# A Conformer convolution's taps moved from GpSimd to VectorE, with its place, its memory and the order of four merges changed

## The chip, the cores and the metric

The kernel runs on one core of one Trainium2 chip. The time is that of one execution on the device, in microseconds, from the slowest (here the only) core; lower is better. Of the engines, TensorE (PE) multiplies matrices into PSUM, VectorE (DVE), ScalarE (ACT) and GpSimd (POOL) work element by element, and SyncE (SP) issues most of the DMAs. Each engine takes its instructions in the order in which the built program has them, and waits on semaphores for the others.

## The reference, cut to what matters

One layer of a trunk, 256 latent and 256 context tokens, 2048 channels. One wide input projection feeds four parallel token mixers of 512 channels; their outputs are projected back, weighted with sigmoid gates, added, and sent through one output projection. A gated ConvFFN follows.

```python
def conv_module(u, p):
    a, gte = jnp.split(u, 2, axis=-1)
    y = a * jax.nn.sigmoid(gte)
    y = dwconv1d(y, p['conv_dw']) + p['conv_b']          # 31 taps, 512 channels, 256 tokens
    y = layer_norm(y, p['conv_ln_g'], p['conv_ln_b'], NORM_EPS)
    return jax.nn.silu(y)

def merge_branches(ys, gate_cols, w_br, w_out):
    ys = jnp.stack([y.astype(dt) for y in ys], axis=2)   # convolution, mLSTM, DeltaNet, RWKV
    br = jnp.einsum('btnw,nwd->btnd', ys, w_br)
    gates = jax.nn.sigmoid(gate_cols.reshape(*gate_cols.shape[:2], N_BRANCH, -1))
    return jnp.sum(gates * br, axis=2) @ w_out
```

The four branches enter a sum, so the order in which they are merged is free.

## The kernel before

**Matrix products.** Every product with a large weight is made from three matmuls. A block of weights of 256 rows and 512 columns (512 KB) comes by DMA into a tile `raw` (four buffers, `load_split`, L194). ScalarE rounds it to a tile `hi` (L198), VectorE writes the remainder into a tile `lo` (L200, called "a `lo`" below), and TensorE adds hi with hi, hi with lo and lo with hi of the activations `uh` and `ul`, which all go through the helper line L79. `hi` and `lo` have two buffers each. So a step of a weight product can only start when VectorE has written its `lo`. The PSUM tile of a product that has the tokens as rows is named `psA`, with the tokens as columns `psB`; a pool of four banks (`mmp`) holds them.

**The order of the work.** The code is written function by function, and the build then places every instruction in a fixed order for each engine by a simulated timeline; work written later goes forward into gaps of work written earlier, where its data and its memory allow it. So the function that is written first has precedence, not the right to finish first. In the region that the change touches, `build` writes: `rw_out` (RWKV output), `gd_scan` and `gd_out` (the DeltaNet scan and its output), `conv_module`, `ml_scan` (the mLSTM scan with its output), `gates` (the 8192 gate columns, 128 steps of 12 matmuls, no dependence on the scans), four calls of `merge` (branch 3 RWKV, 0 convolution, 2 DeltaNet, 1 mLSTM), `out_proj`, then the FFN. The gates are TensorE's filler for the three scans. The columns of the adaLN projection (`w_mod`, PSUM tile `psw`) are fed in between by `feed`, a fraction of a step after each step of the products; they read one buffer `wraw`.

**conv_module.** The padded input `cpad` is loaded, and four blocks of 128 channels get 31 taps of 256 tokens each into `cacc`. Blocks 0 and 1 are on VectorE, one multiply-add for each tap (L869). Blocks 2 and 3 are on GpSimd, a multiply (L874) and an add (L875) for each tap. Then come the layer norm, whose means over channels are matmuls with a matrix of ones (`pscm`, `pscv`), SiLU, and `put_y` (L778, L779), which splits the result into `uh` and `ul` for the merge.

**The DeltaNet scan** inverts a triangular matrix for each segment and direction: first two small steps (L417, L418), then fifteen rounds of a shuffle (L434), a product (`gim`, L402) and an addition (L403) on VectorE, then a reset (L427). Its masks are made on GpSimd (`gdr`).

**The mLSTM scan** takes four heads and two directions. For each, TensorE makes the exponents' argument (`psr`), ScalarE five exponentials (`mA`, L1254 to L1259), VectorE three products, TensorE the sums (`psn`), and VectorE the quotient (`mlh`). Then `head_out` normalises and splits.

**merge** multiplies one branch by its 2048 columns of `w_br` in four blocks of 512, reads the gates back from DRAM (`sig`), and adds up in `mg`; VectorE multiplies, GpSimd adds (L1347).

**Memory.** Pools are stacks from both ends of the SBUF, and a tile that takes over an address waits until the tile before it there was read for the last time. Before, the mLSTM scan's pool `mrp` (addresses 174144 to 221568) lies over the convolution's pool `cvp` (182912 to 194656), and `mg` lies over the mLSTM tiles `mA`.

Of the kernel before, what the change touches and what calls it, by code (L numbers as in the profile page):

```python
# [11 lines left out]
F32 = mybir.dt.float32  # L12
# [3 lines left out]
AF = mybir.ActivationFunctionType  # L16
ALU = mybir.AluOpType
# [3 lines left out]
P = 128  # L21
D = 2048
# [19 lines left out]
class Kern:  # L42
# [812 lines left out]
    def conv_module(self):  # L855
        nc, PC = self.nc, self.PC
        cp = self.cvp
        cpad = cp.tile([P, 4, 286], F32, name="cpad")
# [3 lines left out]
        acc = cp.tile([P, 4, 256], F32, name="cacc")  # L862
        w = lambda i, t: PC["conv_dw"][:, 4 * t + i : 4 * t + i + 1]
        for i in range(4):
            a = acc[:, i]
            if i < 2:
                nc.vector.tensor_scalar(a, cpad[:, i, 0:256], w(i, 0), PC["conv_b"][:, i : i + 1], ALU.mult, ALU.add)
                for t in range(1, 31):
                    nc.vector.scalar_tensor_tensor(a, cpad[:, i, t : t + 256], w(i, t), a, ALU.mult, ALU.add)  # L869
            else:  # L870
                nc.gpsimd.tensor_scalar(a, cpad[:, i, 0:256], w(i, 0), PC["conv_b"][:, i : i + 1], ALU.mult, ALU.add)
                for t in range(1, 31):
                    m = cp.tile([P, 256], F32, tag="ctap", name="ctap", bufs=2)
                    nc.gpsimd.tensor_scalar(m, cpad[:, i, t : t + 256], w(i, t), None, ALU.mult)  # L874
                    nc.gpsimd.tensor_tensor(a, a, m, ALU.add)  # L875
        ps = self.aux("pscm")
# [5 lines left out]
        for i in range(4):  # L882
            nc.vector.tensor_tensor(acc[:, i], acc[:, i], mean, ALU.subtract)
            sq = cp.tile([P, 256], F32, tag="ctap", name="csq", bufs=2)
            nc.gpsimd.tensor_tensor(sq, acc[:, i], acc[:, i], ALU.mult)
            self.mm(ps2[:, 0:256], self.ones, sq, start=i == 0, stop=i == 3)
# [132 lines left out]
    def gd_scan(self):  # L1019
# [4 lines left out]
        wp = self.pool("gwp", bufs=2, stack=ges, side="right")  # L1024
        self.G[0] = self.pool("g1p", stack=self.ues).tile([P, D], F32, name="G1")
        tp = self.pool("gtp", stack=ges, side="right")
# [156 lines left out]
    def ml_scan(self):  # L1183
# [4 lines left out]
        wp = self.pool("mwb", bufs=2, stack=self.mlx)  # L1188
        mqT, mkT = mp.tile([P, 4, 256], F32, name="mqT"), mp.tile([P, 4, 512], F32, name="mkT")
        mv = mp.tile([P, 4, 4, 132], F32, name="mv")  # L1190
# [354 lines left out]
    def build(self):  # L1545
# [46 lines left out]
        res.close()  # L1592
        ces = ExitStack()
        self.gop = self.pool("gop", stack=ces, side="right")
        self.cvp = self.pool("cvp", stack=ces, side="right")
        self.gd_scan()
        self.gd_out()
        self.conv_module()
        ces.close()
        self.ml_scan()  # L1600
        self.gates()
        self.feed(96)
        self.rate = 0.0
        fes.close()
        self.dbg("yh", self.uh[:, :, 0:256].bitcast(F32))
        self.dbg("yl", self.ul[:, :, 0:256].bitcast(F32))
        self.mgw = self.pool("mgw", bufs=3, stack=ues)
        self.mgp = self.pool("mgp", stack=ues)
        self.mg = self.mgp.tile([P, 2, D], F32, name="mg")
        self.hlp = self.pool("hlp", bufs=2, stack=ues)  # L1610
        self.resp = self.pool("resp", side="right")
        self.x1 = self.resp.tile([P, 2, D], F32, name="x1")
        self.ffdw = self.resp.tile([P, 396], F32, name="ffdw")
        self.nc.sync.dma_start(out=self.ffdw, in_=self.A["taps"])
        for i, n in enumerate((3, 0, 2, 1)):
            self.merge(i == 0, n)
# [69 lines left out]
```

## Time and profile before

| what | us |
|---|---|
| median of 3 runs | 2329.57 (2326.28 to 2334.89) |
| the profiled execution | 2329.05 |
| its span, first to last instruction | 2327.1 |
| granted TensorE clock, mean of the span | 0.977 |
| taps on VectorE (L869), first to last start | 789.1 to 848.7 |
| taps on GpSimd (L874), first to last start | 789.0 to 947.7 |
| means of the convolution (`pscm`), first start | 1210.6 |
| its last split (`ul`, L779), start | 1233.1 |

The stages in the span: RWKV scan and the columns of the branches up to some 765 us, the gates with the three scans up to 1317, the four merges from 1342 to 1454, the output projection to 1521, and the FFN to the end. The profile's page gives the shares of the engines and the span in 40 slices of 58 us; a question about less than such a slice goes to the windows, the timeline and the groups of instructions, which the prediction quotes. Busy time of TensorE is modelled (matmuls overlap), so a short wait can be hidden in it.

### The profile page before, as it was taken

To read this page: it belongs to the slowest core of one execution; us is meant where nothing else is said; L and a number is where in the kernel's file an instruction comes from. 1 tells how busy PE (TensorE), PEld (TensorE's weight loads), DVE (VectorE), ACT (ScalarE), POOL (GpSimd) and SP (SyncE) were. 2 spreads that over 40 slices of the span, in tenths; PEclk is the share of its full clock that TensorE was granted. 3 is DMA by queue.
4 is the path that set the end of the run, shared out by engine and by line. 5 is a ranking of instruction groups with operands and counts; after the bars stand their busy time and mean duration, and the time that the engine had idled before them with its cause. 6 is when DMAs were issued, how large, how long until landed. Compare 5 with 4: busy or idle time off the path is not lost.

```text
span 2327.1 us, 42867 instructions
## 1 busy us (share of the span) xinstructions
PE 2215.9 (95%) x16828; PEld 1812.0 (78%) x16828; DVE 1449.6 (62%) x3027; ACT 989.5 (43%) x1493; POOL 507.6 (22%) x865
## 2 busy tenths in 40 slices
PE   6979889999999989999999899989999999999998
PEld 3657667877888666777777678779999999998886
DVE  3357766734555678457565476577776677775554
ACT  4225644533554344334236434444443444444443
POOL 0012553533454599210010033010000000000000
PEclk8989999999999999999999999989999999999999
DMA  9934663555666776787777476567677666666663
GB/s 369 352 115 127 170 183 113 159 171 170 199 188 180 231 208 209 231 247 237 226 231 256 139 257 217 181 231 222 212 222 217 202 182 183 179 205 202 194 193 101
DMA packets 273867, 471.97 MB, mean 203 GB/s; under 512 B 41761, under 2 KB 80929, under 8 KB 272673
## 3 DMA queue, kind: packets, MB, share of 16 engines
q1 hardware_dynamic: 273378, 467.14, 64.8%
q8 instruction: 132, 2.16, 0.4%
q10 hardware_dynamic: 288, 2.10, 0.2%
q14 instruction: 69, 0.57, 0.1%
HBM read 440.33 MB, written 28.84 MB: 202 GB/s over the span
## 4 chain that ended last, share of the span: by engine, by line
PE 78%; DVE 8%; DMA 7%; POOL 4%; ACT 2%; issue 2%; SPq 0%; DVEq 0%; ACTq 0%; POOLq 0%
PE psB L79 37%; PE psA L79 18%; PE psD L79 10%; PE psw L79 4%; DMA wraw<-in_w_mod 3%; DVE lo L200 2%; POOL ctap L874 1%; DMA raw<-in_w_mix 1%; PE psG L79 1%; POOL cacc L875 1%; ACT hi L198 1%; PE psn L79 1%; DMA raw<-in_w_in 1%; PE psf L79 1%; DVE cacc L869 1%
## 5 line engine op out<-in xcount | busy, mean ns | idle before, releaser
L200 DVE TENSOR_TENSOR lo<-raw,hi 128x1024 fp32r<-128x1024 f32 (+2 forms) x485 | 599.2, 1236 | 458.7 <-ACT hi L198 450.0
L198 ACT ACTIVATE hi<-raw 128x1024 fp32r<-128x1024 f32 (+2 forms) x488 | 509.2, 1045 | 796.5 <-PE psB L79 348.6
L79 PE MATMUL psB<-u2h,hi 128*128 128x256 f32 x1408 | 399.5, 286 | 1.2 <-DVE u2h L1370 1.2
L79 PE MATMUL psB<-u2l,hi 128*128 128x256 f32 x1408 | 398.8, 284 | 0.5 <-DVE u2l L1371 0.5
L79 PE MATMUL psB<-u2h,lo 128*128 128x256 f32 x1408 | 399.0, 284 | 0.0
L79 PE MATMUL psA<-lo,uh 128*128 128x512 f32 x832 | 337.4, 406 | 18.4 <-DVE lo L200 18.0
L79 PE MATMUL psA<-hi,ul 128*128 128x512 f32 x832 | 332.7, 400 | 0.0
L79 PE MATMUL psA<-hi,uh 128*128 128x512 f32 x832 | 311.4, 405 | 3.2 <-DVE mg L1344 2.1
L79 PE MATMUL psB<-uh,hi 128*128 128x256 f32 (+1 forms) x832 | 281.0, 346 | 18.7 <-ACT hi L198 16.4
L79 PE MATMUL psB<-ul,hi 128*128 128x256 f32 (+2 forms) x832 | 278.5, 339 | 0.0
L79 PEld LDWEIGHTS psB<-u2h,hi 128*128 128x128 f32 x1408 | 269.6, 192 | 10.9 <-issue 9.5
L79 PEld LDWEIGHTS psB<-u2l,hi 128*128 128x128 f32 x1408 | 270.5, 192 | 0.7 <-DVE u2l L1371 0.7
L79 PE MATMUL psB<-uh,lo 128*128 128x256 f32 (+2 forms) x832 | 263.0, 339 | 8.1 <-DVE lo L200 8.1
L79 PEld LDWEIGHTS psB<-u2h,lo 128*128 128x128 f32 x1408 | 270.5, 192 | 0.1
L79 PEld LDWEIGHTS psA<-lo,uh 128*128 128x128 f32 x832 | 158.1, 190 | 68.5 <-DVE lo L200 27.5
L79 PEld LDWEIGHTS psB<-uh,hi 128*128 128x128 f32 x832 | 158.6, 191 | 51.2 <-ACT hi L198 18.5
L79 PEld LDWEIGHTS psA<-hi,uh 128*128 128x128 f32 x832 | 154.7, 190 | 53.2 <-issue 12.2
L79 PEld LDWEIGHTS psA<-hi,ul 128*128 128x128 f32 x832 | 158.3, 190 | 36.5 <-issue 2.6
L79 PEld LDWEIGHTS psB<-uh,lo 128*128 128x128 f32 (+1 forms) x832 | 152.8, 189 | 32.0 <-DVE lo L200 10.5
L79 PEld LDWEIGHTS psB<-ul,hi 128*128 128x128 f32 (+1 forms) x832 | 157.8, 190 | 23.1 <-issue 6.4
L1541 DVE TENSOR_TENSOR lo<-raw,hi 128x1024 fp32r<-128x1024 f32 x88 | 107.7, 1226 | 78.5 <-ACT hi L1540 78.5
L1461 DVE SCALAR_TENSOR_TENSOR facc<-fpad,ffdw,facc 128x256 f32<-128x256 f32 x352 | 152.8, 490 | 0.2
(573 smaller groups left out, 3028.8 us busy)
## 6 DMA issues: line engine op xcount, KB each, us to landing
raw<-in_w_in SPq DMA_DIRECT2D x208, 512.0 KB, 4.3
raw<-in_ffn_up SPq DMA_DIRECT2D x176, 512.0 KB, 3.8
wraw<-in_w_mod SPq DMA_DIRECT2D x160, 512.0 KB, 5.1
raw<-in_ffn_down SPq DMA_DIRECT2D x88, 512.0 KB, 4.5
raw<-in_w_br SPq DMA_DIRECT2D x32, 512.0 KB, 5.1
raw<-in_w_out SPq DMA_DIRECT2D x32, 512.0 KB, 4.4
raw<-in_w_mod SPq DMA_DIRECT2D x32, 512.0 KB, 3.8
raw<-in_w_in SPq DMA_DIRECT2D x48, 256.0 KB, 4.1
```

The costliest lines, as they stand in the source:

```text
L79: self.nc.tensor.matmul(out, lhsT, rhs, start=start, stop=stop)
L198: nc.scalar.activation(hi[s], raw[s], AF.Copy)
L200: (nc.gpsimd if self.pool_lo >= 0 else nc.vector).tensor_tensor(lo[s], raw[s], hi[s].bitcast(F32), ALU.subtract)
L869: nc.vector.scalar_tensor_tensor(a, cpad[:, i, t : t + 256], w(i, t), a, ALU.mult, ALU.add)
L874: nc.gpsimd.tensor_scalar(m, cpad[:, i, t : t + 256], w(i, t), None, ALU.mult)
L875: nc.gpsimd.tensor_tensor(a, a, m, ALU.add)
L1461: nc.vector.scalar_tensor_tensor(s3(acc), pad[:, dy : dy + 4, dx : dx + 64], tap(t, b), s3(acc), ALU.mult, ALU.add)
L1541: nc.vector.tensor_tensor(f(lo), f(raw), f(hi).bitcast(F32), ALU.subtract)
```

## The change

All four blocks of taps are one multiply-add for each tap on VectorE; GpSimd keeps none. The squares for the variance move from GpSimd to ScalarE. `conv_module` is written behind `gates` instead of behind `gd_out`, its pool stays open until then, and the merges run in the order 3, 2, 1, 0, so that the convolution's branch comes last. In memory, `mqT` and `mkT` of the mLSTM scan get a pool of their own, G1 (the gain of the first residual) is allocated behind the mLSTM scan and not in the DeltaNet scan, `resp` and `hlp` are opened ahead of the merge buffers, and `ffdw` is eight columns wider. The addresses that follow: `mrp` lies at 190560 to 225696 and `cvp` at 178816 to 190560, apart from each other; `x1` (from 178304) now lies over `cvp`.

```diff
@@ conv_module
-            if i < 2:
-                nc.vector.tensor_scalar(a, cpad[:, i, 0:256], w(i, 0), PC["conv_b"][:, i : i + 1], ALU.mult, ALU.add)
-                for t in range(1, 31):
-                    nc.vector.scalar_tensor_tensor(a, cpad[:, i, t : t + 256], w(i, t), a, ALU.mult, ALU.add)
-            else:
-                nc.gpsimd.tensor_scalar(a, cpad[:, i, 0:256], w(i, 0), PC["conv_b"][:, i : i + 1], ALU.mult, ALU.add)
-                for t in range(1, 31):
-                    m = cp.tile([P, 256], F32, tag="ctap", name="ctap", bufs=2)
-                    nc.gpsimd.tensor_scalar(m, cpad[:, i, t : t + 256], w(i, t), None, ALU.mult)
-                    nc.gpsimd.tensor_tensor(a, a, m, ALU.add)
+            nc.vector.tensor_scalar(a, cpad[:, i, 0:256], w(i, 0), PC["conv_b"][:, i : i + 1], ALU.mult, ALU.add)
+            for t in range(1, 31):
+                nc.vector.scalar_tensor_tensor(a, cpad[:, i, t : t + 256], w(i, t), a, ALU.mult, ALU.add)
...
-            nc.gpsimd.tensor_tensor(sq, acc[:, i], acc[:, i], ALU.mult)
+            nc.scalar.activation(sq, acc[:, i], AF.Square)
@@ gd_scan
-        self.G[0] = self.pool("g1p", stack=self.ues).tile([P, D], F32, name="G1")
@@ ml_scan
-        mqT, mkT = mp.tile([P, 4, 256], F32, name="mqT"), mp.tile([P, 4, 512], F32, name="mkT")
+        qk = self.pool("mqk", stack=self.mlx)
+        mqT, mkT = qk.tile([P, 4, 256], F32, name="mqT"), qk.tile([P, 4, 512], F32, name="mkT")
@@ build
         ces = ExitStack()
+        cvs = ExitStack()
+        self.cvp = self.pool("cvp", stack=cvs, side="right")
         self.gop = self.pool("gop", stack=ces, side="right")
-        self.cvp = self.pool("cvp", stack=ces, side="right")
         self.gd_scan()
         self.gd_out()
-        self.conv_module()
         ces.close()
         self.ml_scan()
+        self.G[0] = self.pool("g1p", stack=ues).tile([P, D], F32, name="G1")
         self.gates()
         self.feed(96)
         self.rate = 0.0
+        self.conv_module()
+        cvs.close()
         fes.close()
...
+        self.resp = self.pool("resp", side="right")
+        self.hlp = self.pool("hlp", bufs=2, stack=ues)
         self.mgw = self.pool("mgw", bufs=3, stack=ues)
         self.mgp = self.pool("mgp", stack=ues)
         self.mg = self.mgp.tile([P, 2, D], F32, name="mg")
-        self.hlp = self.pool("hlp", bufs=2, stack=ues)
-        self.resp = self.pool("resp", side="right")
         self.x1 = self.resp.tile([P, 2, D], F32, name="x1")
-        self.ffdw = self.resp.tile([P, 396], F32, name="ffdw")
-        self.nc.sync.dma_start(out=self.ffdw, in_=self.A["taps"])
-        for i, n in enumerate((3, 0, 2, 1)):
+        self.ffdw = self.resp.tile([P, 404], F32, name="ffdw")
+        self.nc.sync.dma_start(out=self.ffdw[:, 0:396], in_=self.A["taps"])
+        for i, n in enumerate((3, 2, 1, 0)):
             self.merge(i == 0, n)
```

What the build makes of it is seen in three places. First VectorE under the taps, between the first and the second `royf` rows of the RWKV output and on. Before (`x6` is six rows of the kind in a row):

```order
L1312 TENSOR_TENSOR royf<-royf,psgo 128x256
L869 SCALAR_TENSOR_TENSOR cacc<-cpad,vec,cacc 128x256 x3
L200 TENSOR_TENSOR lo<-raw,hi 128x1024
L779 TENSOR_TENSOR ul<-royf,uh 128x256
L869 SCALAR_TENSOR_TENSOR cacc<-cpad,vec,cacc 128x256 x6
L200 TENSOR_TENSOR lo<-raw,hi 128x1024
L869 SCALAR_TENSOR_TENSOR cacc<-cpad,vec,cacc 128x256 x2
L1312 TENSOR_TENSOR royf<-royf,psgo 128x256
L869 SCALAR_TENSOR_TENSOR cacc<-cpad,vec,cacc 128x256 x4
L200 TENSOR_TENSOR lo<-raw,hi 128x1024
L869 SCALAR_TENSOR_TENSOR cacc<-cpad,vec,cacc 128x256
```

In the change, from the first `ul` row of the RWKV output on:

```order
L779 TENSOR_TENSOR ul<-royf,uh 128x256
L868 SCALAR_TENSOR_TENSOR cacc<-cpad,vec,cacc 128x256 x3
L288 TENSOR_TENSOR mod_139<-psf,vec 128x2 x2
L200 TENSOR_TENSOR lo<-raw,hi 128x1024
L868 SCALAR_TENSOR_TENSOR cacc<-cpad,vec,cacc 128x256 x3
L1305 TENSOR_TENSOR royf<-royf,psgo 128x256
L868 SCALAR_TENSOR_TENSOR cacc<-cpad,vec,cacc 128x256 x3
L200 TENSOR_TENSOR lo<-raw,hi 128x1024
L868 SCALAR_TENSOR_TENSOR cacc<-cpad,vec,cacc 128x256 x2
L779 TENSOR_TENSOR ul<-royf,uh 128x256
L868 SCALAR_TENSOR_TENSOR cacc<-cpad,vec,cacc 128x256 x4
```

The taps stand among the `lo` rows in both, at the same place in the program. In the change they go on longer: the last tap stands behind the 24th `lo` from the first tap on, where before the first step of the DeltaNet inverse stands behind the 22nd.

Second, TensorE behind the DeltaNet output (`psho`). Before, the convolution's means come next:

```order
L79 MATMUL psA<-lo,uh 128x512
L79 MATMUL psA<-hi,ul 128x512
L79 MATMUL psA<-hi,uh 128x512
L79 MATMUL psho<-ident,go 128x2x64 x2
L79 MATMUL pscm<-cacc,ones 128x256 x4
L79 MATMUL psA<-lo,uh 128x512
L79 MATMUL psA<-hi,ul 128x512
L79 MATMUL psA<-hi,uh 128x512 x2
```

In the change, at the same place:

```order
L79 MATMUL psA<-hi,ul 128x512
L79 MATMUL psA<-hi,uh 128x512
L79 MATMUL psA<-lo,uh 128x512
L79 MATMUL psho<-ident,go 128x2x64 x2
L90 MATMUL psml<-ident,li 4x128 x4
L79 MATMUL psw<-wraw,cst 32x256
L90 MATMUL psml<-ident,spx 4x128 x4
L79 MATMUL psw<-wraw,cst 32x256 x3
```

The mLSTM scan's preparation (`psml`) stands directly behind the DeltaNet output, between steps of `w_mod`, and the convolution's means stand in the merges, behind the mLSTM output.

Third, TensorE at the end of the mLSTM scan, from where the first two blocks of the merge of branch 3 have been multiplied. Before:

```order
L79 MATMUL psq_11528<-mqT,mkT 128x256 x2
L79 MATMUL psn<-mv,mA 128x129 x5
L79 MATMUL psq_11529<-mqT,mkT 128x256 x2
L79 MATMUL psr<-mlr_11292,mlsel 128x256 x2
L79 LDWEIGHTS idb
L79 MATMUL psr<-mlmask,idb 128x256
L79 MATMUL psn<-mv,mA 128x129 x7
L79 MATMUL psr<-mlr_11324,mlsel 128x256 x2
L79 LDWEIGHTS idb
L79 MATMUL psr<-mlmask,idb 128x256
L79 MATMUL psn<-mv,mA 128x129 x7
L79 MATMUL psA<-hi,uh 128x512
```

In the change:

```order
L79 MATMUL psA<-hi,ul 128x512
L79 MATMUL psr<-mlr_10998,mlsel 128x256 x2
L79 LDWEIGHTS idb
L79 MATMUL psr<-mlmask,idb 128x256
L79 MATMUL psw<-wraw,cst 32x256 x4
L79 MATMUL psf<-wrows,selb 128x256 x2
L79 MATMUL psn<-mv,mA 128x129 x7
L79 MATMUL psr<-mlr_11030,mlsel 128x256 x2
L79 LDWEIGHTS idb
L79 MATMUL psr<-mlmask,idb 128x256
L79 MATMUL psn<-mv,mA 128x129 x7
L79 MATMUL psA<-hi,uh 128x512
```

Before, three pairs of a `psr` and the `psn` that needs it are left when the merge has no free PSUM bank (the `psr` of the first stands three rows ahead of this piece); in the change two are left, and the last step of `w_mod` stands among them.

## The prediction

> **What bounds the kernel now.** The profile's page comes first, for the share of each engine, then the table of windows, for the stages that the change touches.
>
> ```profile
> PE 2215.9 (95%) x16828; PEld 1812.0 (78%) x16828; DVE 1449.6 (62%) x3027; ACT 989.5 (43%) x1493; POOL 507.6 (22%) x865
> ```
>
> TensorE is busy for 95% of the span, so a change that moves no matmul work off it can win only time in which it waits, or runs at a lowered clock. In the windows the columns are length, PE, PEld, DVE, ACT and POOL busy, granted clock, DMA share, GB/s:
>
> ```profile
> 788.00:885.00 97.00, 86.14 (x492) 60.09 (x491) 77.21 (x114) 37.23 (x51) 93.13 (x91) 0.96 0.72 211
> 885.00:938.00 53.00, 46.47 (x400) 32.06 (x400) 49.94 (x152) 20.42 (x27) 49.64 (x51) 0.96 0.70 209
> 938.00:961.00 23.00, 22.43 (x263) 16.47 (x263) 8.51 (x9) 9.19 (x13) 7.51 (x9) 0.94 0.77 228
> 961.00:1308.00 347.00, 344.15 (x2510) 253.51 (x2506) 202.10 (x445) 144.67 (x194) 26.13 (x27) 1.00 0.77 234
> 1308.00:1342.00 34.00, 24.74 (x112) 19.11 (x110) 13.15 (x33) 10.63 (x28) 0.70 (x1) 0.80 0.27 95
> 1342.00:1373.00 31.00, 29.27 (x120) 22.68 (x121) 23.94 (x43) 11.02 (x13) 7.45 (x6) 0.94 0.74 269
> ```
>
> While the taps run (788 to 938) TensorE idles 10.9 + 6.5 us, 0.6 more to 961, and its clock is lowered by 4 to 6%, which is 3.9 + 2.1 + 1.4 = 7.4 us of clock. After that it waits 2.9 us in 347: there nothing is to be won. The hole from 1308 to 1342 (the end of the mLSTM scan) holds 9.3 us of idling, the first merges 1.7.
>
> **Why TensorE idles under the taps.** Two groups of VectorE work between 788 and 850, two of GpSimd between 780 and 960 (busy, mean ns):
>
> ```profile
> L869 DVE SCALAR_TENSOR_TENSOR cacc<-cpad,vec,cacc 128x256 f32<-128x256 f32 x60 | 38.5, 684 | 0.0
> L200 DVE TENSOR_TENSOR lo<-raw,hi 128x1024 fp32r<-128x1024 f32 x14 | 19.5, 1395 | 0.0
> L874 POOL TENSOR_SCALAR ctap<-cpad,vec 128x256 f32<-128x256 f32 x60 | 76.8, 1289 | 0.0
> L875 POOL TENSOR_TENSOR cacc<-cacc,ctap 128x256 f32<-128x256 f32 x60 | 55.9, 931 | 1.7
> ```
>
> VectorE holds the 60 taps of two channel blocks and the `lo` halves without which the gates' matmuls cannot start. GpSimd takes 132.7 us for the other 60. A tap costs VectorE 38.5/60 = 0.64 us here. In the FFN, where GpSimd rests, the same operation of the same size looks like this (start, length of the merged run), and below it the same 56-element step of the DeltaNet inverse (in the tile name `gim`), first with GpSimd's taps running, then without:
>
> ```profile
> 1572.71 1.22 DVE L200 TENSOR_TENSOR lo<-raw,hi 128x1024 fp32r<-128x1024 f32 x1
> 1573.85 1.27 DVE L1461 SCALAR_TENSOR_TENSOR facc<-fpad,ffdw,facc 128x256 f32<-128x256 f32 x3
> ...
> 1588.96 2.47 DVE L1461 SCALAR_TENSOR_TENSOR facc<-fpad,ffdw,facc 128x256 f32<-128x256 f32 x6
> 899.46 0.74 DVE L402 TENSOR_TENSOR gim<-gib,giU 128x56 f32<-128x56 f32 x1
> 1061.52 0.21 DVE L402 TENSOR_TENSOR gim<-gib,giU 128x56 f32<-128x56 f32 x1
> ```
>
> Three more taps take 2.47 - 1.27 = 1.20 us, so a tap costs 0.40 us, and a `lo` costs 1573.85 - 1572.71 = 1.14 us. A step of 0.21 us takes 0.74 us beside GpSimd. So the two engines hold each other up, and the taps slow VectorE even where they run on GpSimd. The Trainium skill, page "SBUF — State Buffer", section "Who interferes with whom", says that a VectorE instruction with two SBUF inputs and a GpSimd instruction that reads SBUF shut each other out for a whole instruction. By that rule GpSimd's other work in the three windows, 150.3 - 132.7 = 17.6 us, would go on blocking VectorE, and term A below would be anything up to 17.6 us less; by the rows it is as below, and I keep the rows.
>
> **Term A, the taps (788 to 961).** By the order of the built programs the taps still start at the same place, not behind the gates. 60 taps join VectorE, 120 operations leave GpSimd. Up to the first step of the inverse, at 884.90 in this trace, VectorE had 22 `lo` rows; in the change it has 24, two steps of the gates further.
>
> ```profile
> 884.90 0.36 DVE L417 TENSOR_SCALAR giA<-giC,mlo 128x128 f32<-128x128 f32 x1 [0.31 <-ACT giC L94]
> 910.53 0.18 DVE L427 COPY giU<-I 128x128 f32<-128x128 f32 x1
> 1050.24 0.29 DVE L417 TENSOR_SCALAR giA<-giC,mlo 128x128 f32<-128x128 f32 x1 [0.78 <-ACT giC L94]
> 1069.06 0.19 DVE L427 COPY giU<-I 128x128 f32<-128x128 f32 x1
> 1378.52 33.51 PE psA L79 x144
> ```
>
> - VectorE's sum: 120 x 0.40 + 24 x 1.14 + 4 opening taps at 0.40 + the rest of that stretch, about 77.2 - 38.5 - 19.5 - 8 x 1.3 = 9 us: 48.0 + 27.4 + 1.6 + 9 = 86 us, so 874.
> - TensorE's sum: 86.1 us busy, less the 3.9 of lowered clock, plus two steps of 12 matmuls at 33.51/144 = 0.233 us (the chain of waits), 5.6 us: 87.8 us, so 876.
>
> The two are nearly equal and take turns, so I put the inverse at 880: 4.9 us earlier and 5.6 us of gates further, 10.5 us. The first inverse took 910.53 - 884.90 = 25.6 us against 18.8 us in the second segment, where GpSimd is quiet. There TensorE becomes the limit (46.5 us busy, 2.1 of them lowered clock, in 53), and I count 5 us for both directions. **Term A is -15 us.** Its ends: all idling and all lowered clock go, -18.0 - 7.4 = -25; or a tap still costs 0.64 us, then VectorE has 115 us to the inverse, which starts at 903 with 5.6 us of gates more done: +12.5.
>
> **Term B, the end of the mLSTM scan.** It has two parts. First, in the old layout the scan's memory lay over the convolution's:
>
> ```profile
> POOL mv L1191 <- DVE ul L779: 13.9, 1, 13.9
> 1317.12 1.13 PE L79 MATMUL psr<-mlr,mlsel 4*128 4x256 f32 x4
> 1325.83 0.45 PE L79 MATMUL psr<-mlr,mlsel 4*128 4x256 f32 x1 [0.60 <-DVE mlh L1280]
> 1332.65 2.04 PE L79 MATMUL psr<-mlr,mlsel 4*128 4x256 f32 x4 [1.47 <-DVE mlh L1278]
> 1342.25 0.50 PE L79 MATMUL psA<-hi,uh 128*128 128x512 f32 x1 [2.09 <-DVE mg L1344]
> 1320.28 1.20 PE L79 MATMUL psn<-mv,mA 128*128 128x129 f32 x4 [1.82 <-DVE mA L1261]
> ```
>
> GpSimd's `mv` waited 13.9 us for the last `ul` of the convolution, and the scan's loads stand behind it. In the change the scan starts right behind the DeltaNet output. Second, the merge of branch 3 fills four PSUM banks and then stops until the scan is over; three psr-to-psn pairs are left at that point before, two in the change. The first of the three runs from 1317.12 to 1325.83, 8.7 us, but its matmuls are not saved, they move into the busy gates. What goes is its idling, 1.8 + 0.6 = 2.4 us. **Term B is -2.5 us**; at best the whole 8.7 us, at worst nothing, if the scan is late by its own chain.
>
> **Term C, the convolution's ending.** Means, squares, reciprocal, SiLU and splits leave the stage with 2.9 us of idling in 347 and come into the first merges:
>
> ```profile
> 1213.06 2.27 DVE L883 TENSOR_TENSOR cacc<-cacc,cmean 128x256 f32<-128x256 f32 x4 [0.75 <-ACT cmean L880]
> 1222.24 1.28 ACT L888 ACT_TABLE_LOAD   x1
> 1224.69 1.75 DVE L889 RECIPROCAL crt<-crt 128x256 f32<-128x256 f32 x1 [1.21 <-ACT crt L888]
> 1226.55 1.43 DVE L891 TENSOR_TENSOR cacc<-cacc,crt 128x256 f32<-128x256 f32 x4
> 1226.63 1.28 ACT L892 ACT_TABLE_LOAD   x1
> 1357.12 2.12 ACTq L1420 DMA_DIRECT2D x<-in_x  x2
> 1359.53 10.60 DMA raw<-in_w_br
> ```
>
> With four splits of 0.33 that is 2.27 + 1.75 + 1.43 + 1.3 = 6.8 us of VectorE, put where VectorE is busy 23.9 of 31 us already: 30.7. The cover is nearly used up. The squares move from GpSimd to ScalarE, which has room there (11.0 of 31). The 2 MB of `x` are queued on ScalarE behind this ending, since `x1` now lies over the convolution's memory; today they collide with the merges' weights (10.6 us for a load at 1359), later they will again. SP's loads of `w_mod` move too: more of them stand between the last gate weights and the first merge weights. They run in the scan's hole, where the DMA share is 0.27, so I count nothing for them, at most one load. Ends: 0, if the 7 us of VectorE slack are enough; +9.4, if 6.8 us and both table loads are exposed. I take **+3 us**, nearer the rows that say there is room. The new place of G1, the wider `ffdw` and the order of merges 2, 1 and 0 issue the same instructions at the same prices: 0.
>
> **The sum.** -15 - 2.5 + 3 = -14.5 us on the profiled execution of 2329.05 us (span 2327.1), which is 0.5 us from the median of the runs: 2314.5, and I forecast **2314 us**. 0.5% is 11.6 us, about what a measurement of this kernel can tell from no change.
>
> **The rivals.**
> - *VectorE becomes the bound (slower).* The taps cost 0.64 us whatever GpSimd does. Then A is +12.5, and the sum 2329 + 12.5 - 2.5 + 3 = 2342. The point from which A turns is where 788.3 + 38 + 120 taps reaches 884.9 + 5.6: 0.535 us a tap. For it: VectorE is the saturated engine (no idling in the 62 us to 850). Against it: 0.40 us in the FFN, 0.21 against 0.74 us in the inverse. The Trainium skill, page "Perfetto Trace Analysis", section "Optimizing Scalar/DVE Operations", advises giving work of a saturated VectorE away, even to GpSimd, and so speaks against this change; it adds that the shared port may undo that, and the 0.74 us row sides with the second half.
> - *Only the inverse gains.* VectorE and TensorE do not take turns well while the taps run, and 10.9 us of idling stay: A is -5 - 2.5 of clock, the sum 2329 - 7.5 - 2.5 + 3 = 2322.
> - *The merges give it back.* C is +9.4: 2329 - 15 - 2.5 + 9.4 = 2321. For it: the 30.7 of 31 us. Against it: the ending spreads over some 13 steps of 2.8 us.
> - *All of it goes.* A -25, C 0: 2329 - 25 - 2.5 = 2301.5.
>
> **How the numbers follow.** Forecast 0.50 (its own range 2308 to 2319), only the inverse 0.16, the merges 0.16, all of it 0.10, VectorE bound 0.08. Faster by over 0.5% (below 2317.9): 0.45 of the forecast, 0.10 of the best case, 0.04 of the two middle ones, 0.59. Slower by over 0.5%: 0.07. Within: 0.34. The range that leaves out about 2 in 10 runs from 2303, near the best case, to 2327, above the middle ones.
>
> **What would show it.** Taps at 0.40 us and inverse steps near 0.2 us; the inverse starting near 880 with 24 `lo` before it; idling from 788 to 961 down from 18 to some 8 us, clock near 0.98; `mv` no longer waiting for `ul`; two pairs in the hole; and in the 31 us behind it VectorE near 30 with TensorE idling some 4 us in place of 1.7. It is wrong if a tap takes over 0.53 us, or if the merges' `lo` rows come later than every 2.8 us.

## The result, and the profile after

The changed kernel takes **2315.48 us** (median of 4 runs, 2314.22 to 2316.15) beside 2328.28 us of the kernel before; the ratio is **0.9944** with a 95% interval of 0.9932 to 0.9957. A second set of six runs gave 0.9943 (0.9926 to 0.9959). So it is faster by 13 us, about 0.56%, and the interval reaches to both sides of the 0.5% that was named as the bound. The forecast was 2314 us.

First the share of each engine on the page of the changed kernel, then its windows, with the columns of before; the first three are the stretches that the prediction quoted.

```profile
PE 2216.0 (96%) x16828; PEld 1810.1 (78%) x16828; DVE 1448.9 (63%) x3089; ACT 990.7 (43%) x1498; POOL 374.2 (16%) x739
```
```profile
788.00:885.00 97.00, 93.90 (x558) 66.83 (x557) 94.11 (x186) 40.98 (x55) 21.54 (x25) 1.00 0.80 249
885.00:938.00 53.00, 51.08 (x554) 36.95 (x553) 39.35 (x150) 23.20 (x30) 1.09 (x3) 1.00 0.81 249
938.00:961.00 23.00, 23.00 (x205) 16.57 (x205) 9.97 (x17) 9.94 (x15) 0.00 (x0) 1.00 0.75 216
961.00:1283.50 322.50, 320.76 (x2306) 234.24 (x2303) 186.77 (x423) 130.88 (x175) 18.80 (x22) 1.00 0.74 226
1283.50:1318.24 34.74, 28.10 (x142) 21.13 (x141) 14.02 (x29) 12.70 (x26) 2.22 (x2) 0.85 0.58 186
1318.24:1433.90 115.66, 111.02 (x491) 89.51 (x492) 85.66 (x118) 51.83 (x74) 42.65 (x28) 0.99 0.69 234
```

Under the taps TensorE now idles 3.1 + 1.9 + 0 = 5.0 us in place of 18.0, and GpSimd is busy for 22.6 us in place of 150.3. The last two rows are the hole from the last gate to the restart of the merges, and the merges up to the output projection. The same two stretches before (there the gates end at 1300.1; what TensorE multiplies from then to 1317 are mostly the first blocks of the merge of branch 3):

```profile
1300.10:1342.25 42.15, 32.64 (x153) 25.85 (x152) 16.33 (x39) 14.26 (x33) 0.95 (x1) 0.84 0.38 125
1342.25:1451.70 109.45, 107.87 (x476) 86.62 (x477) 76.97 (x105) 43.76 (x58) 41.71 (x26) 0.98 0.74 247
```

The hole is shorter (34.7 after 42.2 us), the merges are longer (115.7 after 109.5), and TensorE idles in them 4.6 us in place of 1.6. From these and the later milestones of the two traces the difference adds up:

| up to | before | after | step |
|---|---|---|---|
| restart of the merges (first `psA` behind the hole) | 1342.25 | 1318.24 | -24.0 |
| first `mg` of the output projection | 1451.7 | 1433.9 | +6.2 |
| last residual of the attention half (`x`, an1ry) | 1526.2 | 1510.3 | +1.9 |
| end of the span | 2327.1 | 2313.7 | +2.5 |

24 us are won before the merges, and 10.6 are given back behind them: in the merges, and, unexpectedly, in the output projection and the FFN. A second profiled execution of the same program has +0.5 and +1.0 us in these last two rows in place of +1.9 and +2.5, so a part of them is chance: in the output projection the granted clock was 0.97 in the first execution and 1.00 in the second.

The taps and the inverse in the changed kernel: a group of VectorE from 788 to 884, two single rows, and a group from 885 to 905 (busy, mean ns).

```profile
L868 DVE SCALAR_TENSOR_TENSOR cacc<-cpad,vec,cacc 128x256 f32<-128x256 f32 x120 | 57.1, 524 | 0.0
```
```profile
883.57 0.28 DVE L417 TENSOR_SCALAR giA<-giC,mlo 128x128 f32<-128x128 f32 x1 [1.44 <-ACT giC L94]
902.49 0.19 DVE L427 COPY giU<-I 128x128 f32<-128x128 f32 x1
L402 DVE TENSOR_TENSOR gim<-gib,giU 128x120 f32<-128x120 f32 (+14 forms) x16 | 3.5, 220 | 0.0
```

A tap costs VectorE 57.1/120 = 0.476 us (0.64 before, 0.40 predicted). The inverse starts at 883.6, with the predicted 24 `lo` rows ahead of it, and its first piece takes 902.49 - 883.57 = 18.9 us in place of 25.6. GpSimd's `mv` now waits for the end of the DeltaNet output (`psho`) and not for the convolution's `ul`:

```profile
L1184 POOL MEMSET mv<- x1: 127/127/127, 1191.5 to 1191.5; 128x16 f32 x1
its engine sat idle before it (us, times) until:
  PE psho L79: 15.9, 1
```

Last, the merges of the changed kernel in slices of 10 us, and VectorE in and ahead of the third of them (start, length):

```profile
1327.00:1337.00 10.00, 10.00 (x50) 8.33 (x49) 9.38 (x18) 4.08 (x8) 0.00 (x0) 1.00 0.76 242
1337.00:1347.00 10.00, 10.00 (x46) 8.24 (x45) 6.48 (x9) 6.24 (x9) 3.53 (x2) 1.00 0.66 217
1347.00:1357.00 10.00, 6.96 (x31) 5.36 (x30) 10.00 (x14) 7.01 (x12) 3.39 (x3) 1.00 0.47 156
1357.00:1367.00 10.00, 9.63 (x42) 7.56 (x41) 8.01 (x8) 3.94 (x4) 6.45 (x4) 1.00 0.94 358
```
```profile
1344.84 1.22 DVE L200 TENSOR_TENSOR lo<-raw,hi 128x1024 fp32r<-128x1024 f32 x1 [2.02 <-ACT hi L198]
1346.63 1.75 DVE L882 RECIPROCAL crt<-crt 128x256 f32<-128x256 f32 x1 [0.56 <-ACT crt L881]
1348.30 1.22 DVE L1339 TENSOR_TENSOR sig<-sig,psA 128x512 f32<-128x512 f32 x2
1349.44 3.22 DVE L884 TENSOR_TENSOR cacc<-cacc,crt 128x256 f32<-128x256 f32 x4
1352.58 2.35 DVE L200 TENSOR_TENSOR lo<-raw,hi 128x1024 fp32r<-128x1024 f32 x2
```

Between 1347 and 1357 VectorE has no gap, TensorE idles 3.0 us, and even the transfers pause (DMA share 0.47), because a weight buffer comes free only when its `lo` is written (between 1340 and 1362 the queue of the weight loads waits 13.8 us for `lo` rows): the reciprocal and the four products of the convolution's norm stand between two `lo` rows that are 6.5 us apart (1344.84 + 1.22 to 1352.58). The four products take 3.22 us here, 1.43 before.

### The profile page after: what moved, and what is told of

It reads as the page before. It is cut to its first block, busy times and chain, and to the rows that moved or that the text cites. A ratio compares the mean times of both kernels' runs of the same rounds, so it can differ in the third digit from the quotient of the medians.

```text
span 2313.7 us, 42812 instructions
## 1 busy us (share of the span) xinstructions
PE 2216.0 (96%) x16828; PEld 1810.1 (78%) x16828; DVE 1448.9 (63%) x3089; ACT 990.7 (43%) x1498; POOL 374.2 (16%) x739
## 4 chain that ended last, share of the span: by engine, by line
PE 83%; DVE 6%; DMA 5%; ACT 2%; issue 1%; POOL 1%; SPq 0%; DVEq 0%; ACTq 0%; POOLq 0%
PE psB L79 38%; PE psA L79 21%; PE psD L79 10%; PE psw L79 4%; DMA wraw<-in_w_mod 3%; DVE lo L200 2%; DMA raw<-in_w_mix 1%; PE psG L79 1%; DVE cacc L868 1%; ACT hi L198 1%; PE psn L79 1%; PE psf L79 1%; PE psSA L79 1%; PE psY L79 0%; PE pd L79 0%
```

## The experiments

Two theories were open. **By the first**, GpSimd's half of the taps held VectorE up, and the three terms of the prediction add. **By the second**, the gain needs the new place and memory, or comes from them. The kernels below differ from the one named by the edit alone. The milestones are starts in the profiled execution of each (`sig` of the last gates, first `psr` and last `psn` of the mLSTM scan, first `mg` of the merges and of the output projection); the times are medians, the ratios to the kernel before with it on the same chip. The profiled execution took 5.6 us more than the median in e1, 7.1 us less in e9, and within 3.1 us of it in the others, so a single milestone is no better than that.

| kernel | last gate | first psr | last psn | merges | out proj | us | ratio (95%) |
|---|---|---|---|---|---|---|---|
| before | 1300.1 | 1252.4 | 1339.7 | 1341.5 | 1451.7 | 2328.3 | |
| changed | 1283.5 | 1212.6 | 1315.7 | 1317.5 | 1433.9 | 2315.5 | 0.9944 (0.9932-0.9957) |
| e1 taps alone | 1282.8 | 1242.9 | 1329.6 | 1331.3 | 1443.7 | 2315.6 | 0.9955 (0.9941-0.9969) |
| e2 changed, GpSimd keeps its taps | 1301.6 | 1227.2 | 1327.4 | 1329.2 | 1446.6 | 2326.7 | 0.9996 (0.9987-1.0006) |
| e3 changed, convolution written early | 1290.0 | 1224.9 | 1321.3 | 1323.1 | 1432.5 | 2309.2 | 0.9925 (0.9912-0.9939) |
| e4 taps alone, GpSimd loaded for nothing | 1308.5 | 1272.5 | 1355.5 | 1357.3 | 1466.5 | 2340.7 | 1.0064 (1.0049-1.0079) |
| e5 layout alone | 1307.2 | 1237.2 | 1337.1 | 1338.9 | 1448.5 | 2326.0 | 0.9989 (0.9976-1.0001) |
| e8 taps and layout | 1283.4 | 1220.2 | 1317.4 | 1319.2 | 1427.8 | **2306.5** | **0.9910** (0.9895-0.9925) |
| e7 changed, norm off VectorE | 1284.9 | 1213.9 | 1317.5 | 1319.3 | 1432.9 | 2310.3 | 0.9923 (0.9909-0.9936) |
| e6 ending inside the scan | 1287.7 | 1211.7 | 1320.7 | 1322.4 | 1431.6 | 2308.9 | 0.9920 (0.9906-0.9934) |
| changed, again | 1284.2 | 1213.3 | 1316.8 | 1318.6 | 1436.8 | 2315.5 | 0.9943 (0.9926-0.9959) |
| e11 e8, ffdw narrow | 1283.7 | 1220.0 | 1316.5 | 1318.3 | 1427.7 | 2313.3 | 0.9936 (0.9923-0.9950) |
| e9 e8, w_mod fed slower | 1275.0 | 1228.0 | 1321.8 | 1323.6 | 1434.9 | 2318.9 | 0.9961 (0.9947-0.9975) |

**e1: the taps alone.** Before, with the loop of the change:

```diff
-            if i < 2:
...
-                    nc.gpsimd.tensor_scalar(m, cpad[:, i, t : t + 256], w(i, t), None, ALU.mult)
-                    nc.gpsimd.tensor_tensor(a, a, m, ALU.add)
+            for t in range(1, 31):
+                nc.vector.scalar_tensor_tensor(a, cpad[:, i, t : t + 256], w(i, t), a, ALU.mult, ALU.add)
```

> The kernel before, with nothing changed but the taps: all 120 multiply-adds on VectorE, none on GpSimd. The convolution stays where it was written, the memory, the squares and the order of the merges stay. Theory 'GpSimd held VectorE up': the whole gain of the taps comes from this one edit, since the idling of 18 us and the lowered clock of 7.4 us between 788 and 961 us come from the two engines blocking each other. Then a tap costs 0.40 to 0.48 us, idling there is 5 us or less, the clock is near 1.00, and the time is 2328 - 20 = 2308 us (2303 to 2313); being without the convolution's ending in the merges it would be ahead of the changed kernel (2315.5). Rival 'the place does it' (the gain needs the convolution written behind the gates and the memory laid out apart): 2322 us or more.

2315.6 us: between the two ranges, 2.6 us above the first. Idling from 788 to 961 is 6.6 us, a tap 0.47 us, and the last gate is as early as in the changed kernel, as the first theory says. But of these 17 us only 10 reach the merges:

```profile
L1319 ACT ACTIVATE sig<-psA x12: 591/597/600, 1113.1 to 1282.8; 128x512 f32<-128x512 f32 x12
L1184 POOL MEMSET mv<- x1: 126/126/126, 1223.7 to 1223.7; 128x16 f32 x1
  DVE ul L779: 18.2, 1
L79 PE MATMUL psr<-mlr,mlsel x32: 374/374/762, 1242.9 to 1324.3; 4*128 4x256 f32 x32
L1337 DVE TENSOR_TENSOR mg<-sig,psA x8: 679/680/687, 1331.3 to 1346.0; 128x512 f32<-128x512 f32 x8
```

In these rows of e1 (smallest, median and largest length, first and last start; the row under `mv` is what GpSimd waited for before it) `mv` still waits for the convolution's `ul`, 18.2 us, until 1223.7, and the scan ends 48.5 us behind the last gate (1282.8 to 1331.3, against 41.4 before). With the gates shorter, the scan is late.

**e2: the changed kernel, with blocks 2 and 3 of the taps on GpSimd.** The inverse of the edit of e1, on the changed kernel.

> The changed kernel, but with blocks 2 and 3 of the taps on GpSimd as before; place, memory, squares on ScalarE and order of the merges are those of the change. Theory 'GpSimd held VectorE up': taps cost VectorE 0.64 us again, idling between 788 and 961 is near 18 us, and of the change only the end of the mLSTM scan (-2.5 us) and the loss in the merges (+6 us as the trace of the changed kernel has it) are left: 2328 + 3.5 = 2331 us (2326 to 2335). Rival 'the place does it': 2316 to 2320 us.

2326.7 us, no difference from before, within the first theory's range; idling from 788 to 961 is 19.0 us. Without the taps the rest of the change is worth nothing in sum. Its parts are not those of the theory, though: the merges start 12.3 us earlier than before (the theory had 2.5), they take 117.4 us in place of 110.2, and the FFN's down projection takes 248.7 us in place of 241.8, which no theory had.

**e3: the changed kernel, with the convolution written early.**

```diff
         self.gd_out()
+        self.conv_module()
         ces.close()
...
-        self.conv_module()
         cvs.close()
```

> The changed kernel, with one line moved back: the convolution is written behind the DeltaNet output as before, so that its means, reciprocal, SiLU and splits run in the gates and not in the merges. Taps, memory and order of the merges are those of the change. Theory 'the merges lose to the convolution's ending': the changed kernel gave back 6.3 us of 24 in its merges; here that comes back, the merges take 111 us again from their first mg to the output projection (116.4 in the changed kernel), and the time is 2315.5 - 6 = 2309.5 us (2307 to 2312). Rival 'the merges lose to transfers' (the weights of the merges, of w_mod and the 2 MB of x come closer together since the scan's hole is shorter): 2314 to 2316 us.

2309.2 us, as expected; from the first `mg` to the output projection 109.4 us. The ending costs the merges 7 us. What it costs the kernel is less certain: the intervals of the two ratios overlap, and in e3 the merges start some 5 us later than in the changed kernel. A part of that is chance, since the inverse began at 887.6 us here and at 883.6 us there, with the same order of instructions up to it.

**e4: as e1, with GpSimd at work on 60 taps that nobody reads.**

```diff
+            if i >= 2:
+                for t in range(1, 31):
+                    m = cp.tile([P, 256], F32, tag="ctap", name="ctap", bufs=2)
+                    nc.gpsimd.tensor_scalar(m, cpad[:, i, t : t + 256], w(i, t), None, ALU.mult)
+                    nc.gpsimd.tensor_tensor(m, m, cpad[:, i, t : t + 256], ALU.add)
```

> The kernel before with all 120 taps on VectorE, and GpSimd still does the multiplication and one addition of 60 taps, into buffers that nothing reads: its load is doubled work, VectorE's is that of the change. It changes no other instruction. Theory 'GpSimd held VectorE up': taps on VectorE cost 0.6 to 0.7 us while GpSimd works, VectorE is the bound up to the first DeltaNet inverse, idling between 788 and 961 grows to 30 us or more, and the time is 2336 to 2345 us, above the kernel before. Rival 'VectorE has the room and GpSimd's slow chain only came late': GpSimd's results are waited for by nobody here, so the time is that of the taps on VectorE alone, 2308 to 2314 us.

2340.7 us, within the first theory's range. One window, and the taps from 788 to 910, in e4:

```profile
788.00:961.00 173.00, 146.74 (x959) 101.54 (x957) 162.35 (x331) 63.06 (x83) 150.64 (x146) 0.97 0.70 205
L868 DVE SCALAR_TENSOR_TENSOR cacc<-cpad,vec,cacc 128x256 f32<-128x256 f32 x120 | 71.6, 647 | 0.0
```

The same 120 taps take 71.6 us beside GpSimd's 150.6 us of work, 14.5 more than in the changed kernel, and TensorE idles 26.3 us. Nobody waits for these taps. Work of GpSimd that others need stands behind them in its queue, but from 780 to 1000 the trace has only 4.9 us of waits for it (VectorE 2.8 for `gdr`, ScalarE 1.8 for `gioff`, TensorE 0.3). TensorE waits for `lo`, in e4 and in e1 (us in total, times, longest):

```profile
PE psA L79 <- DVE lo L200: 23.2, 23, 2.9
PE psA L79 <- DVE lo L200: 1.8, 1, 1.8
```

So it is GpSimd's running that costs, some 25 us between e1 and e4.

**e5 and e8: the layout alone, and the layout with the taps.** Both have the memory of the change, the convolution written early as in e3, squares on GpSimd and merges 3, 0, 2, 1; e5 has the taps of before, e8 those of the change. Against the changed kernel, e8 is:

```diff
         self.gd_out()
+        self.conv_module()
         ces.close()
...
-        self.conv_module()
         cvs.close()
...
-            nc.scalar.activation(sq, acc[:, i], AF.Square)
+            nc.gpsimd.tensor_tensor(sq, acc[:, i], acc[:, i], ALU.mult)
...
-        for i, n in enumerate((3, 2, 1, 0)):
+        for i, n in enumerate((3, 0, 2, 1)):
```

> The kernel before with nothing changed but the memory: the mLSTM scan's pool apart from the convolution's, mqT and mkT in a pool of their own, G1 and the merge buffers as in the change. Taps half on GpSimd, convolution written early, squares on GpSimd, merges 3, 0, 2, 1. Theory 'the scan is a limit of its own' (its end, not the end of the gates, starts the merges, so an earlier scan is worth its own microseconds): the layout alone gives what lies between the runs with the taps on VectorE (written early in the new layout 2309, in the old one 2315.6): 2328 - 6 = 2322 us, with mv no longer waiting for ul and the first psr some 15 us earlier. Rival 'the layout pays only when the gates end earlier' (term B as it was predicted, -2.5 us at most): 2325.5 to 2328 us.

> The same as the run of the layout alone, but with all 120 taps on VectorE: taps and memory of the change, while the convolution is written early, its squares stay on GpSimd and the merges run 3, 0, 2, 1. Theory 'the layout': it is the memory that makes the 6.5 us between the taps alone (2315.6) and the run with the convolution written early (2309.2), so the time here is 2309 us (2306 to 2312). Rival 'squares or order of the merges': 2315 us.

e5 is 2326.0 us, in the rival's range: 1.2 us below the kernel before that ran beside it, 2.6 us by the ratio, and its interval reaches 1.0001, so it can't be told from no change. The first `psr` comes 15 us earlier, yet the last `psn` only 2.6; the gates, which share TensorE with the scan, end 7 us later. e8 is **2306.5 us**, faster than both kernels of this study; its interval lies below that of the changed kernel. Its rows against those of e1:

```profile
L1319 ACT ACTIVATE sig<-psA x12: 588/597/599, 1104.8 to 1283.4; 128x512 f32<-128x512 f32 x12
L1184 POOL MEMSET mv<- x1: 128/128/128, 1188.6 to 1188.6; 128x16 f32 x1
L79 PE MATMUL psr<-mlr,mlsel x32: 374/374/760, 1220.2 to 1311.7; 4*128 4x256 f32 x32
L1337 DVE TENSOR_TENSOR mg<-sig,psA x8: 678/680/686, 1319.2 to 1333.0; 128x512 f32<-128x512 f32 x8
```

The gates end where they end in e1, the scan starts 23 us earlier, and the merges 12. So, with the convolution written early, the layout is worth some 2 us with the old taps and 9 us (2315.6 to 2306.5; 10.5 by the ratios) with the new ones. Between e3 and e8 lie squares and the order of the merges, with 2.7 us whose intervals overlap: open.

**e7: the changed kernel without VectorE's part of the layer norm.**

```diff
-            nc.vector.tensor_tensor(acc[:, i], acc[:, i], mean, ALU.subtract)
...
-        nc.vector.reciprocal(rt, rt)
...
-            nc.vector.tensor_tensor(acc[:, i], acc[:, i], rt, ALU.mult)
```

> The changed kernel, with the convolution's layer norm leaving out VectorE's part: the four subtractions of the mean, the reciprocal and the four products with it (5.5 us of VectorE by the trace of before). Means, squares, square root, SiLU and splits stay where they are. Theory 'VectorE is full in the merges': the stretch of 10 us in which VectorE has no gap and TensorE idles 3.0 us goes, the merges take 3 us less, and the time is 2315.5 - 3 = 2312.5 us (2310.5 to 2314). Rival 'transfers' (x and the weights of the merges come too close together): the idling stays within 1 us of what it was, 2315 us.

2310.3 us, 0.2 us below the first theory's range; its interval overlaps that of the changed kernel. The merges take 113.6 us in place of 116.4 (and 118.2 in the repeat), and the stretch with the full VectorE is gone; the slice of 10 us from 1350 in e7, 31 us behind its first `mg`:

```profile
1350.00:1360.00 10.00, 9.47 (x41) 7.08 (x40) 6.77 (x8) 3.52 (x4) 6.10 (x4) 1.00 0.97 352
```

In it x's transfer and the weights still meet (DMA share 0.97), and TensorE idles 0.5 us; over all merges it idles 1.8 us in place of 4.6. So the 3.0 us were VectorE's, not the transfers'. The other 2 us of the gain in the median are not explained by this.

**e6: the ending inside the scan.** e3, with the part from the means on in a function of its own:

```diff
+            if h == 0:
+                self.conv_end()
         self.dbg("mlh", hs)
```

> The run with the convolution written early, but its ending (means to splits) is written inside the mLSTM scan, behind the first head, and no longer ahead of it; the taps stay where they are. Theory 'the ending holds up the scan when written ahead, and the merges when written behind': the first psr comes near 1213 us as in the changed kernel (1225 in the run written early), the merges take 110 us, and the time is 2305 to 2307 us, faster than any run so far. Rival 'the scan has to let the ending through in any case': the last psn is as late as with the ending ahead of the scan (1321 us), 2309 us or more.

2308.9 us: the rival, at the edge of its range. The first `psr` is early (1211.7), but the last `psn` is at 1320.7, as with the ending ahead of the scan (1321.3).

**The changed kernel again, e11 and e9**, all three on one chip.

> The changed kernel itself, on one chip with the two runs beside it, for two questions. First the price of the convolution's ending in the merges: it is the distance to the run with the taps and the layout alone (0.991 of before), by the theory 8 us (2315 us, 0.9945), by the rival that the two were taken at different times and differ by chance 2 to 4 us (2309 to 2311 us). Second, the matmuls of the FFN's down projection started every 229 ns in the profile of the changed kernel and every 227 ns before, with the same order of instructions. If that belongs to the program, it is 229 ns again; if it belongs to the execution, another number.

2315.5 us again (0.9943), so the distance to e8 stands, 7.7 us by the ratios. Next, e8 with the narrow `ffdw` (e11):

```diff
-        self.ffdw = self.resp.tile([P, 404], F32, name="ffdw")
+        self.ffdw = self.resp.tile([P, 396], F32, name="ffdw")
```

> The run with the taps and the layout alone, but with ffdw at its old width of 396 columns, so that the FFN's buffers lie 32 bytes lower (hh at 207456 and not at 207488). It changes no instruction. Theory 'the wider ffdw is free' (as the prediction had it): 2306.5 us again, down projection at 229 ns a matmul. Rival 'the address of hh sets the rate of the down projection': another rate, such as the 227 ns of before (-2.4 us) or the 233 ns that one of the other runs had (+4.5 us).

2313.3 us: the rival, with its 233 ns, though it had 2311 us. It is 6 us behind e8 by the ratios, with the same instructions in the same order on all engines. Windows of 190 us in the down projection, in this order before, the changed kernel again, e2, e11 (the second number of a row is PE busy, with its matmuls in brackets):

```profile
2106.20:2296.20 190.00, 190.00 (x840) 157.32 (x839) 100.32 (x106) 84.82 (x106) 0.00 (x0) 1.00 0.59 186
```
```profile
2091.80:2281.80 190.00, 190.00 (x832) 155.89 (x831) 99.65 (x104) 83.55 (x103) 0.00 (x0) 1.00 0.56 184
```
```profile
2101.40:2291.40 190.00, 190.00 (x816) 153.91 (x815) 97.44 (x102) 82.55 (x102) 0.00 (x0) 1.00 0.58 185
```
```profile
2084.40:2274.40 190.00, 190.00 (x816) 152.82 (x816) 97.85 (x102) 82.31 (x102) 0.00 (x0) 1.00 0.56 183
```

A matmul every 226, 228 and 233 ns by these counts (the expectations call the first two 227 and 229), always with a busy TensorE at full clock. The changed kernel has the same rate in both its executions, so by this one repeat it belongs to the program. The narrow `ffdw` has the slow rate, so the width is not without effect. Of the 6 us the down projection shows 3.2 (244.1 us in e8, 247.3 in e11, first to last start); another 2.1 us of this trace are in the output projection, where the granted clock was 0.97 in e11 and 1.00 in e8.

Last of the three, e8 with `w_mod` fed more slowly (e9):

```diff
-        self.rate = 0.55
+        self.rate = 0.50
```

> The run with the taps and the layout alone, but with 0.50 in place of 0.55 steps of w_mod fed per step of the products, so that some five small steps of w_mod (0.64 us of TensorE each) are left for the end of the mLSTM scan, where TensorE idles 6.6 us and runs at 0.85 of its clock. Theory 'the hole can be filled with work that has no dependence on the scan': the gates end 3 us earlier, the scan with them, 2303 to 2305 us. Rival 'the last pairs are a chain of their own' (psr, exponentials, products, psn, quotient, with only one buffer for w_mod's weights): the hole stays as long as it was and w_mod's loads stand in its way, 2306 to 2310 us.

2318.9 us, worse than either theory. The gates end 8 us earlier, but the scan starts 8 us later and ends 48.6 us behind the last gate. The hole cannot be filled this way; how the rate delays the scan was not followed up.

## Why the prediction was right, and where it was not

The forecast of 2314 us was right, with a sum of -14.5 us against a measured -13. The mechanism of the taps was right. The sizes of the single terms were not, and their errors cancelled, so it is partly luck that the total came so close.

- **Term A (predicted -15 us).** With the layout of the change and the convolution written early it is 2326.0 to 2306.5, **-19.5 us** (e5 to e8); in the old layout -12.7 by the medians, -10.5 by the ratio (e1); taken out of the changed kernel itself -11.2 (e2), of which 4.6 are the down projection. So the term has no single size. The steps: the inverse starts at 883.6 (880 predicted) with exactly 24 `lo`, its first piece is 6.7 us shorter (5 counted), idling is 5.0 us (8 predicted). A tap is 0.476 us and not 0.40, 120 x 0.076 = 9.1 us more in VectorE's sum, but below the 0.535 us from which A would turn. The 0.40 came from six taps in a row; all 352 taps of the FFN before take 152.8 us, 0.434 each, which is nearer. The rival "VectorE becomes the bound" was worked out at 2342 us; e4, in which GpSimd goes on working, is at 2340.7. The rule of the Trainium skill, page "SBUF — State Buffer", section "Who interferes with whom", by which GpSimd's remaining work would go on blocking VectorE for up to 17.6 us, shows as at most these 9.1 us. The Trainium skill's page "Perfetto Trace Analysis", section "Optimizing Scalar/DVE Operations", says that giving work of a saturated VectorE even to GpSimd may make sense; here it did not, by e1 and e4, and the page's own doubt about the shared port is borne out.
- **Term B (predicted -2.5 us).** Alone it measured -1.2 us by the medians and -2.6 by the ratio (e5). `mv` waits for `psho`, and two pairs are left in the hole, as predicted. What failed is the step that **added A and B as if each could be had alone**. A shortens the gates, and the scan then sets the start of the merges: without B, A is about 7 us smaller (12.7 for 19.5), and behind A, B is worth 9 us and not 2. By the ratios the two together win 8 us more than the sum of each alone, with an uncertainty of some 5.6 us (from the three intervals). The price of B had to be taken at the gates' new end, not the old one. Nor does B stand apart from the place of the convolution: with the old taps the merges start 2.6 us earlier than before when it is written early (e5), 12.3 us when it is written late (e2).
- **Term C (predicted +3 us).** Behind the new taps it measured **+7.7 us** (e8 to the changed kernel, by the ratios, whose intervals nearly touch; squares and order of the merges are in it), near the upper end of 9.4. Against e3, which differs by the place alone, it is 4 us by the ratios and 6 by the medians. Behind the old taps the same step is +0.7 us by the medians, +1.6 by the ratios (e5 to e2): there the merges also take 7.8 us more, but start 9.7 us earlier. The argument that the ending spreads over 13 steps fell: reciprocal and products come as one block between two `lo`, the products beside GpSimd's `mg` additions take 3.22 us and not 1.43, and VectorE is full for 10 us. The merges of e8 take 107.9 us, 7.8 less than those of the changed kernel, and TensorE idles 2.0 us in them, 2.6 less. Another 4.1 us are the matmuls of the means and squares, which the prediction moved without counting (the window of e8's merges, and two groups of TensorE in the changed kernel's merges, busy and mean ns):

```profile
1319.91:1427.80 107.89, 105.87 (x476) 85.47 (x477) 77.44 (x105) 43.64 (x58) 43.33 (x28) 1.00 0.75 251
L79 PE MATMUL pscv<-csq,ones 128*128 128x256 f32 x8 | 2.2, 378 | 0.0
L79 PE MATMUL pscm<-cacc,ones 128*128 128x256 f32 x8 | 1.9, 379 | 0.0
```

  They left the gates (from the inverse to the last gate 399.9 and 398.4 us in the two executions of the changed kernel, 403.1 in e8), yet the merges start only 0.6 to 1.7 us earlier than in e8. Part of that is chance: up to the inverse the order of the instructions is the same, and it began at 883.6 and 885.8 in the changed kernel and at 880.3 in e8. The rival "the merges give it back" (C +9.4) thus came nearer for its term than the forecast, while A made up for it.
- **The terms at 0.** New addresses and the wider `ffdw` were priced at nothing. The down projection runs at 228 ns a matmul in place of 226, which is 2.3 us from its first to its last start (241.8 before, 244.1 in both executions of the changed kernel), and 32 bytes less cost e8 another 3.2 us there (e11).
- **The clock.** The 7.4 us of lowered clock under the taps were counted as winnable at the far end alone. The changed kernel's second profiled execution shows 0.96 between 788 and 885, the first (above) 1.00. Its window, and the opening taps of the first and of the second execution:

```profile
788.00:885.00 97.00, 91.69 (x531) 65.36 (x530) 90.70 (x174) 37.74 (x50) 20.23 (x24) 0.96 0.77 234
L866 DVE TENSOR_SCALAR cacc<-cpad,vec x4: 406/406/412, 789.4 to 790.3; 128x256 f32<-128x256 f32 x4
L866 DVE TENSOR_SCALAR cacc<-cpad,vec x4: 407/410/414, 786.5 to 787.4; 128x256 f32<-128x256 f32 x4
```

  From the first opening tap to the inverse the first takes 94.2 us (789.4 to 883.6), the second 99.3 (786.5 to 885.8). With the same order of instructions up to there, e8 has 93.9 us at a clock of 1.00 and e3 99.2 us at 0.96. So the lowered clock of the kernel before is there again in the second execution and in e3, and goes with 5 us in that stretch. What lowers it is not shown.

## What to carry to other kernels

When two chains share a bottleneck engine and a third stage waits for both, price each edit at the end that the other edit leaves behind: here the layout was worth some 2 us alone and 9 us behind the faster taps, and the late ending cost about 1 us behind the old taps and 7.7 behind the new. Count moved work on every engine, the small matmuls too, and look at how a block of it lands between the instructions that feed TensorE, not at the average share of the stage. The element-wise load on GpSimd was paid on VectorE too; what shows it is a run that has GpSimd's work in it, with results that nobody reads.

## What the runs showed of the hardware

- GpSimd's work slows VectorE even where nobody reads its results: a tap costs 0.476 us with little of it (in the changed kernel GpSimd is busy for 21.5 of 97 us) and 0.597 us with it (e4), a 56-element step of the inverse 0.21 and 0.74 us (before).
- In the hole the same matmuls take nearly twice as long once TensorE has waited. In e8, two pairs of the scan, the first of each kind in the busy gates, the second at the end, and the windows of that end with the granted clock (the third number from the end):

```profile
1283.24 1.73 PE L79 MATMUL psn<-mv,mA 128*128 128x129 f32 x14
...
1292.07 1.12 PE L79 MATMUL psr<-mlr,mlsel 4*128 4x256 f32 x4
...
1310.32 2.04 PE L79 MATMUL psr<-mlr,mlsel 4*128 4x256 f32 x4 [1.47 <-DVE mlh L1271]
1312.29 0.39 PE L79 MATMUL psr<-mlmask,idb 128*128 128x256 bf16 x1
1314.47 3.35 PE L79 MATMUL psn<-mv,mA 128*128 128x129 f32 x14 [1.79 <-ACT mA L1252]
```
```profile
1310.30:1312.40 2.10, 2.08 (x5) 1.25 (x5) 0.00 (x0) 0.00 (x0) 0.00 (x0) 0.50 0.00 0
1314.40:1317.90 3.50, 3.35 (x14) 3.08 (x14) 0.62 (x2) 0.04 (x1) 0.00 (x0) 0.50 0.00 0
```

  1.12 us became 2.04, 1.73 became 3.35, at a granted clock of 0.50. The Trainium skill, page "TensorE: Matmul & The Clock Gate", section "Part 1: The HAM clock gate (the "warmup" mystery)", has an idle array run at half its clock; the rows agree.
- The rate of the down projection takes three values, 226, 228 and 233 ns a matmul, in programs whose TensorE order there is the same, and it repeats: 226 in before, e1 and e4 (old layout), 228 in the changed kernel twice and in e3, e5, e6, e7, e8 and e9, 233 in e2 and e11. The FFN's buffers lie at other addresses in the two layouts and in e11, but e2 has those of the changed kernel, so the address alone is not the cause. It stays open, and is worth up to 7 us of 2300.
